# In each chunk of a state chain, the state's part of the outputs is multiplied in front of the solution instead of behind the remainders

## The chip, the cores and the metric

The kernel runs on one core of one Trainium2 chip. The metric is the device time of one execution in microseconds. Inputs and outputs are float32; matrices lie in DRAM and the output must agree with the reference below.

## The reference

One layer of a decoder trunk on a sequence of 1024 tokens with 1024 channels. Three branches (causal pooling, a delta-rule recurrence, cross-attention) share one input projection, are merged by gates and projected, and a feed-forward layer with a causal convolution follows. The change touches the recurrence alone:

```python
def rwkv7_scan(r, w, k, v, kk_neg, kk_a):
    ...
    def step(state, inp):
        rt, wt, kt, vt, an, bn = inp
        sa = jnp.einsum('bhvk,bhk->bhv', state, an)
        state = state * wt[:, :, None, :] + sa[..., None] * bn[:, :, None, :] + vt[..., None] * kt[:, :, None, :]
        yt = jnp.einsum('bhvk,bhk->bhv', state, rt)
        return state, yt
```

It runs for 16 heads of 64 channels. `state` is a 64x64 matrix for each head, and each token updates it and reads it.

## The kernel before

Channels lie on the 128 partitions and tokens along the free dimension. Projections are made with three matmuls of 128x512 for each pair of a weight block and an input block: operands are split into a high and a low part (`whi`, `wlo` for weights, `hh`, `hl` for the input), and `mm3` (L164) multiplies high by high (L167), high by low (L168) and low by high (L169) into a PSUM bank `psg`.

The recurrence runs over four groups of four heads (`rwkv_group`, L432). In a group, `i` (0, 1) counts blocks of 128 partitions, each with two heads: one on partitions 0 to 63 (`lo`), one on 64 to 127 (`up`). Tokens are cut into 16 chunks of 64. Preparation makes for each chunk a few 64x64 matrices: `AR` (scaled readers and keys), `NT` (the inverse of the chunk's triangular system), `RB` and `BKN`. Then the state chain (L645 to L691) goes through the chunks in order, and each step needs the state that the step before left in `HV`:

1. `pr`: four small matmuls of `AR` and `HV` give the remainders (right-hand sides) of the chunk's system, 128 rows deep and 64 columns wide (64 rows deep in the first chunk). VectorE copies them from PSUM to `Rs` (L662).
2. `py<-AR,HV`: from the second chunk on, four small matmuls give the state's part of the chunk's outputs, 64 rows deep and 64 columns wide. They open an accumulation in the PSUM tile `py`.
3. `pu<-Rs,NT`: four small matmuls, 64x64 as well, give the solution. VectorE copies the lower half to `HV` (L665), ScalarE the upper half (L666).
4. `ph<-HV,BKN`: four small matmuls for the next state, which VectorE adds to the decayed old one `Hd` into the next chunk's `HV` (L683) and again into `Hn` (L688), from which ScalarE makes the next `Hd` (L690).
5. `py<-RB,HV`: four small matmuls that complete the outputs; ScalarE copies `py` into `AR` (L691).

All these products are issued by `visit` (L636), so that line L639 stands for each of them in the profile; the tile names tell them apart. In the profile each of them appears as eight records, two for each of the four matmuls. `HV` of a chunk is complete before its `pr` starts, so `py<-AR,HV` waits for nothing that `pr` has not waited for.

The order of instructions on each engine is fixed when the program is built: a scheduler takes them by priority and data dependencies. `later` (L207) adds a dependency that sets this order but makes no engine wait, and `visit` chains its products with it, each behind the one before, the first behind `after`. Where the next small products are not ready yet by the scheduler's reckoning, it takes large matmuls of a projection that has no part in the chain: those of the next group's keys and values, or of the pooling, query and gate columns. So TensorE's queue in the chain is a mixture of rows of small products and single `psg` matmuls. PSUM tiles for `pr`, `pu` and `ph` come in turn from two banks (`bank`, L632), `py` from a pool of two.

Of the kernel before, what the change touches and what calls it, by code (L numbers as in the profile page):

```python
# [9 lines left out]
F32 = mybir.dt.float32  # L10
# [7 lines left out]
P = 128  # L18
# [3 lines left out]
C = 64  # L22
# [22 lines left out]
def trunk_kernel(ctx: ExitStack, tc: tile.TileContext, xT, memT, pvec, w_in, w_kv, w_upd, w_upg,  # L45
                 w_pool, w_ppool, w_pmem, w_prwkv, w_o, w_fup, w_fdn, out):
    nc = tc.nc
    V, A, G, PE, SP = nc.vector, nc.scalar, nc.gpsimd, nc.tensor, nc.sync
# [158 lines left out]
    def later(i, ins, plain=False):  # L207

        tc.add_manual_dep(i if plain else i.ins, ins.name, nosync, reason="order")
# [5 lines left out]
    rw = rw_ctx.enter_context(tc.tile_pool(name="rw", bufs=1))  # L215
# [7 lines left out]
    for k in range(KC):  # L223
        tag = ("X01", "X11", "HV", "HV")[k // 2]
# [207 lines left out]
    def rwkv_group(g, kv):  # L432
# [88 lines left out]
        NT = rw.tile([P, 2, NCH, C], F32, name="NT", tag="NT")  # L521
# [17 lines left out]
        for i in range(2):  # L539
            us = slice(NCH * i, NCH * i + NCH)  # L540
            for c0 in range(0, NCH, 4):
# [3 lines left out]
                lo, up = slice(0, 64), slice(64, 128)  # L545
# [81 lines left out]
        lo, up = slice(0, 64), slice(64, 128)  # L627
# [4 lines left out]
        def bank(name):  # L632
            turn[0] ^= 1
            return (psc if turn[0] else psk).tile([P, 2, C], F32, name=name, tag="c" if turn[0] else "k")

        def visit(products, after):  # L636

            for (out_, l, r), kw in products:
                m = PE.matmul(out_, l, r, **kw)  # L639
                if after is not None:  # L640
                    later(m, after)
                after = m.ins
            return after

        ready = None  # L645
        for c in range(NCH):
            t = slice(c * C, (c + 1) * C)
            once = dict(start=True, stop=True)
            pr = bank("pr")
            py = pss.tile([P, 2, C], F32, name="py", tag="s")  # L650
            ke, ko = (up, lo) if c == 0 else (slice(0, P), slice(0, P))
            row = []
            for i in range(2):
                row.append(((pr[up, i], AR[ko, i, 2, t], HV[ko, i, c, 1]), once))
                row.append(((pr[lo, i], AR[ke, i, 0, t], HV[ke, i, c, 0]), once))
            for i in range(2 if c else 0):
                kw = dict(start=i == 0, stop=False)
                row.append(((py[lo, i], HV[lo, i, c, 0], AR[lo, i, 1, t]), kw))
                row.append(((py[up, i], HV[up, i, c, 1], AR[up, i, 1, t]), kw))
            visit(row, ready)  # L660
            Rs = rw.tile([P, 2, C], F32, name="Rs", tag="Rs", bufs=1)
            V.tensor_copy(Rs, pr)  # L662
            pu = bank("pu")
            visit([((pu[q, i], NT[q, i, c], Rs[q, i]), once) for i in range(2) for q in (lo, up)], None)
            V.tensor_copy(HV[lo, :, c, 0], pu[lo])  # L665
            ready = A.copy(HV[up, :, c, 1], pu[up]).ins  # L666
            row = []
            if c + 1 < NCH:
                ph = bank("ph")
                for i in range(2):  # L670
                    row.append(((ph[up, i], BKN[i][:, c, 64:128], HV[:, i, c, 1]), once))
                    row.append(((ph[lo, i], BKN[i][:, c, 0:64], HV[:, i, c, 0]), once))
            for i in range(2):
                kw = dict(start=c == 0 and i == 0, stop=i == 1)
                row.append(((py[lo, i], HV[:, i, c, 0], RB[i][:, 0, c]), kw))
                row.append(((py[up, i], HV[:, i, c, 1], RB[i][:, 1, c]), kw))
            visit(row, ready)
            if c + 1 < NCH:
                for q, e in ((lo, 0), (up, 1)):
                    if c == 0:  # L680
                        ready = V.tensor_copy(HV[q, :, 1, e], ph[q]).ins
                    else:
                        ready = V.tensor_tensor(HV[q, :, c + 1, e], ph[q], Hd[q], op=ALU.add).ins  # L683
                if c + 2 < NCH:
                    if c == 0:
                        V.tensor_copy(Hn, ph)
                    else:
                        V.tensor_tensor(Hn, ph, Hd, op=ALU.add)  # L688
                    for i in range(2):
                        A.activation(Hd[:, i], Hn[:, i], AF.Identity, scale=Dc[:, i, c + 1:c + 2])  # L690
            A.copy(AR[:, :, 1, t], py)  # L691
# [40 lines left out]
    for g in range(4):  # L732
        kv = rwkv_group(g, kv)
# [113 lines left out]
    for hd in range(4):  # L847
        for t0, _ in HALVES:
            s = slice(t0, t0 + 512)
            q = as_.tile([P, 512], F32, name="q", tag="q", bufs=2)  # L850
# [5 lines left out]
            for u in range(2):  # L856
# [7 lines left out]
                pr = as_.tile([P, 2, 256], F32, name="prb", tag="prb", bufs=2)  # L864
# [742 lines left out]
```

## Time and profile before

| | us |
|---|---|
| median of 3 runs | 2088.79 |
| lowest and highest run | 2087.73, 2090.97 |
| span of the profiled execution | 2088.0 |
| first and last copy L662 (start in the span) | 236.4, 971.8 |

The profiled execution is one more execution; its span, from the first to the last instruction, is the time that the profile has for it. The four chains lie at about 236 to 311, 458 to 533, 681 to 756 and 902 to 975 us of it. Between them TensorE works on the preparation of the next group and on projections; the merge and the feed-forward layer come after the last.

In the profile, PE stands for TensorE's matmuls and PEld for its weight loads, DVE for VectorE, ACT for ScalarE, POOL for GpSimd. A row of a timeline has the start in us, the time from the first start to the last end, the engine, the line, the operation, output and operands by the program's names, the part of the array that is used (rows\*columns), and the shape. The end of a matmul is modelled and contains its way through the array, so that ends overlap the next starts; the time from start to start is what one costs in a full queue. What a row waited for stands in brackets behind it: "issue" is time in which the profile shows nothing waited for.

### The profile page before, as it was taken

The numbers are of one execution on the slowest core, as the hardware profiler recorded it, in microseconds if no ns is written. First come the engines' busy times: TensorE is split into PE (matmuls) and PEld (weight loads), VectorE is DVE, ScalarE is ACT, GpSimd is POOL, SyncE is SP. The second block draws the span as 40 slices with busy tenths as digits, with TensorE's granted clock in tenths as the row PEclk, the third lists the DMA queues.
The fourth block names the chain that finished last, engine by engine and source line by source line (L and its number), as shares of the span: only waits on it lengthen the run. The fifth ranks groups of instructions, "written<-read, shape, count | busy, mean of one in ns | idle before, by whom it ended". The sixth has DMA issues, their size and how long they took to land.

```text
span 2088.0 us, 34125 instructions
## 1 busy us (share of the span) xinstructions
PE 2032.2 (97%) x12246; PEld 1560.9 (75%) x12246; DVE 1358.1 (65%) x2167; ACT 1070.7 (51%) x2252; POOL 812.8 (39%) x917
## 2 busy tenths in 40 slices
PE   8999999999999999999999999998999999999997
PEld 5777767776778667876878878776788877777886
DVE  6567437654667357833695442669877777777798
ACT  7584348623773358434566243545444444444644
POOL 5521213121222121211122355565578888842341
PEclk9999999999999999999999999999999999999999
DMA  4312111120212021213526443634322222169766
GB/s 155 130 40 77 64 57 60 66 82 22 87 61 89 30 92 44 84 57 107 184 82 216 128 144 107 219 99 152 95 88 83 81 78 76 61 189 267 165 180 152
DMA packets 176713, 221.83 MB, mean 106 GB/s; under 512 B 16544, under 2 KB 128288, under 8 KB 176544
## 3 DMA queue, kind: packets, MB, share of 16 engines
q1 hardware_dynamic: 163616, 204.44, 30.1%
q0 software_dynamic: 11856, 14.16, 4.2%
q8 instruction: 97, 1.59, 0.3%
q10 hardware_dynamic: 1072, 1.05, 0.1%
q14 instruction: 72, 0.59, 0.1%
HBM read 170.30 MB, written 49.28 MB: 105 GB/s over the span
## 4 chain that ended last, share of the span: by engine, by line
PE 35%; DVE 5%; POOL 4%; DMA 4%; issue 3%; ACT 2%; SPq 1%; POOLq 0%; DVEq 0%; ACTq 0%
PE psg L167 6%; PE psg L168 6%; PE psg L169 6%; PE psf L169 2%; PE psf L168 2%; PE psf L167 2%; PE psd L168 2%; PE psd L169 2%; POOL wt L1025 2%; PE psd L167 2%; DMA R<-d_f 1%; DMA a<-in_w_fup 1%; POOL sm L1010 1%; ACT d L1041 1%; DVE d L1043 1%
## 5 line engine op out<-in xcount | busy, mean ns | idle before, releaser
L131 POOL TENSOR_TENSOR wlo<-wraw,whi 128x256 fp32r<-128x256 f32 x472 | 412.0, 882 | 955.4 <-ACT whi L128 770.0
L167 PE MATMUL psg<-hh,whi 128*128 128x512 f32 x928 | 382.7, 412 | 2.4 <-DVE kv L314 2.4
L169 PE MATMUL psg<-hh,wlo 128*128 128x512 f32 x928 | 379.4, 409 | 0.1
L168 PE MATMUL psg<-hl,whi 128*128 128x512 f32 x928 | 378.7, 408 | 0.0
L128 ACT CAST whi<-wraw 128x256 fp32r<-128x256 f32 x472 | 182.6, 403 | 231.3 <-PE psg L168 112.6
L167 PEld LDWEIGHTS psg<-hh,whi 128*128 128x128 f32 x928 | 174.4, 188 | 46.3 <-DVE kv L314 3.7
L169 PEld LDWEIGHTS psg<-hh,wlo 128*128 128x128 f32 x928 | 174.1, 188 | 46.1 <-POOL wlo L131 5.4
L168 PEld LDWEIGHTS psg<-hl,whi 128*128 128x128 f32 x928 | 174.4, 188 | 43.0 <-issue 3.6
L1025 POOL TENSOR_TENSOR wt<-a,wt 128x256 fp32r<-128x256 f32 x136 | 133.7, 1011 | 30.9 <-ACT wt L1024 30.9
L167 PE MATMUL psd<-f,u 128*128 128x512 f32 x292 | 115.2, 395 | 6.7 <-ACT f L1345 4.3
L168 PE MATMUL psd<-f,u 128*128 128x512 f32 x292 | 114.9, 394 | 0.9 <-DVE f L1349 0.9
L169 PE MATMUL psd<-f,u 128*128 128x512 f32 x292 | 114.2, 392 | 0.2 <-DVE u L1349 0.2
L1025 POOL TENSOR_TENSOR wt<-sm,wt 128x256 fp32r<-128x256 f32 x102 | 106.8, 1066 | 14.6 <-ACT wt L1024 14.6
L169 PE MATMUL psf<-h2h,wt 128*128 128x512 f32 x272 | 107.9, 397 | 0.1
L167 PE MATMUL psf<-h2h,wt 128*128 128x512 f32 x272 | 106.9, 393 | 0.1
L168 PE MATMUL psf<-h2l,wt 128*128 128x512 f32 x272 | 106.8, 393 | 0.0
L1024 ACT CAST wt<-sm 128x256 fp32r<-128x256 f32 x102 | 37.9, 404 | 128.0 <-POOL sm L1010 124.2
L1043 DVE SCALAR_TENSOR_TENSOR d<-z,pv,d 128x1023 f32<-128x1023 f32 x68 | 91.6, 1347 | 12.0 <-ACT d L1041 9.5
L169 PE MATMUL psf<-t,wt 128*128 128x512 f32 x204 | 81.5, 399 | 2.0 <-POOL wt L1025 1.9
L168 PE MATMUL psf<-t,wt 128*128 128x512 f32 x204 | 80.3, 394 | 0.0
L167 PE MATMUL psf<-t,wt 128*128 128x512 f32 x204 | 80.1, 393 | 0.0
L683 DVE TENSOR_TENSOR HV<-ph,Hd 64x128 f32<-64x128 f32 x112 | 32.3, 288 | 71.7 <-PE ph L639 47.6
(422 smaller groups left out, 4749.2 us busy)
## 6 DMA issues: line engine op xcount, KB each, us to landing
wraw<-in_w_in SPq DMA_DIRECT2D x240, 128.0 KB, 2.4
a<-in_w_fup SPq DMA_DIRECT2D x128, 128.0 KB, 2.4
d_zg<-st SPq DMA_DIRECT2D x48, 256.0 KB, 2.7
wraw<-in_w_fup SPq DMA_DIRECT2D x80, 128.0 KB, 2.4
fw<-in_w_fdn SPq DMA_DIRECT2D x33, 256.0 KB, 4.4
fraw<-d_f SPq DMA_DIRECT2D x33, 256.0 KB, 5.3
wraw<-in_w_prwkv SPq DMA_DIRECT2D x64, 128.0 KB, 2.4
wraw<-in_w_o SPq DMA_DIRECT2D x64, 128.0 KB, 2.5
```

Of the source, the lines that this page charges most:

```text
L128: last_whi[0] = A.copy(hi, src).ins
L131: (V if lo_on_dve[0] else G).tensor_tensor(lo, src, hi.bitcast(F32), op=ALU.subtract)
L167: first = PE.matmul(ps, wh, xh, start=start, stop=False)
L168: PE.matmul(ps, wh, xl, start=False, stop=False)
L169: last_mm[0] = PE.matmul(ps, wl, xh, start=False, stop=stop).ins
L683: ready = V.tensor_tensor(HV[q, :, c + 1, e], ph[q], Hd[q], op=ALU.add).ins
L1010: eng.tensor_tensor(out_[u], a[u], b[u], op=op)
L1024: A.copy(w[0][:, us], src[u])
L1025: last_low[0] = G.tensor_tensor(w[1][:, us], src[u], w[0][:, us].bitcast(F32), op=ALU.subtract).ins
L1041: A.activation(d, z, AF.Identity, scale=col("cw2", j), bias=col("cb", j))
L1043: V.scalar_tensor_tensor(d[:, n:], z[:, :T - n], col(cw, j), d[:, n:], op0=ALU.mult, op1=ALU.add)
```

## The change

The four products `py<-AR,HV` are taken out of the row of `pr` and put into the row of `pu`, ahead of it. The row of `pr` now ends with `pr`. The first product of the new row is ordered behind the copy `Rs` (`made`), as an order in the queue and not as a wait; `pu` is now chained behind `py`. In the first chunk, which has no `py<-AR,HV`, `pu` is ordered behind nothing, as before. No product, copy or transfer is added or taken away.

```diff
@@ -653,15 +653,17 @@
             for i in range(2):
                 row.append(((pr[up, i], AR[ko, i, 2, t], HV[ko, i, c, 1]), once))
                 row.append(((pr[lo, i], AR[ke, i, 0, t], HV[ke, i, c, 0]), once))
+            visit(row, ready)
+            Rs = rw.tile([P, 2, C], F32, name="Rs", tag="Rs", bufs=1)
+            made = V.tensor_copy(Rs, pr).ins
+            pu = bank("pu")
+            row = []
             for i in range(2 if c else 0):
                 kw = dict(start=i == 0, stop=False)
                 row.append(((py[lo, i], HV[lo, i, c, 0], AR[lo, i, 1, t]), kw))
                 row.append(((py[up, i], HV[up, i, c, 1], AR[up, i, 1, t]), kw))
-            visit(row, ready)
-            Rs = rw.tile([P, 2, C], F32, name="Rs", tag="Rs", bufs=1)
-            V.tensor_copy(Rs, pr)
-            pu = bank("pu")
-            visit([((pu[q, i], NT[q, i, c], Rs[q, i]), once) for i in range(2) for q in (lo, up)], None)
+            row += [((pu[q, i], NT[q, i, c], Rs[q, i]), once) for i in range(2) for q in (lo, up)]
+            visit(row, made if c else None)
             V.tensor_copy(HV[lo, :, c, 0], pu[lo])
             ready = A.copy(HV[up, :, c, 1], pu[up]).ins
             row = []
```

Line numbers behind L656 grow by two, so that L665, L666, L683 and L691 become L667, L668, L685 and L693; the copy `Rs` (L662) becomes L658.

The order of instructions changes on TensorE only; on the other engines the rows stand in the order of before. TensorE's queue in the second chunk of the first group, as 48 of the 60 chunks have it (`psg` is a large matmul of a projection, the rest are products of the chain):

```order
 L168 MATMUL psg<-hl,whi 128x512
 L639 MATMUL pr<-HV,AR 64x64 x4
+L169 MATMUL psg<-hh,wlo 128x512
 L639 MATMUL py<-AR,HV 64x64 x4
-L169 MATMUL psg<-hh,wlo 128x512
 L639 MATMUL pu<-Rs,NT 64x64 x4
 L167 MATMUL psg<-hh,whi 128x512
```

The large matmul that stood between `py` and `pu` now stands between `pr` and `py`, and `py` stands directly ahead of `pu`. In 12 chunks the scheduler has put four large matmuls there, since VectorE has a longer instruction (L314) ahead of the copy `Rs`. In six of them all four now stand ahead of `py`. TensorE's queue in one of the other six, in the first chain:

```order
 L169 MATMUL psg<-hh,wlo 128x512
 L639 MATMUL pr<-HV,AR 64x64 x4
+L167 MATMUL psg<-hh,whi 128x512
+L168 MATMUL psg<-hl,whi 128x512
+L169 MATMUL psg<-hh,wlo 128x512
 L639 MATMUL py<-AR,HV 64x64 x4
-L167 MATMUL psg<-hh,whi 128x512
-L168 MATMUL psg<-hl,whi 128x512
-L169 MATMUL psg<-hh,wlo 128x512
 L167 MATMUL psg<-hh,whi 128x512
 L639 MATMUL pu<-Rs,NT 64x64 x4
```

Here three large matmuls have moved ahead of `py`, and the fourth stands between `py` and `pu`.

## The prediction

> **What bounds the kernel now.** The page comes first: which engine is full, and whether it is full all the way.
>
> ```profile
> PE 2032.2 (97%) x12246; PEld 1560.9 (75%) x12246; DVE 1358.1 (65%) x2167; ACT 1070.7 (51%) x2252; POOL 812.8 (39%) x917
> ...
> PE   8999999999999999999999999998999999999997
> ```
>
> TensorE is busy for 97% of the span and in the tens of nines almost everywhere; VectorE is at 65%, ScalarE at 51%. So time is saved by whatever makes TensorE's own queue shorter, as long as nothing else becomes late. The change sits in the state chain, which runs four times. The view of busy time by stretch shows the first two of them (237 to 312 and 470 to 535) and the stretch that follows the second:
>
> ```profile
> core 0: us, PE busy (x) PEld busy (x) DVE busy (x) ACT busy (x) POOL busy (x), PEclk, DMA share, GB/s
> ...
> 237.00:312.00 75.00, 75.00 (x949) 50.34 (x949) 26.32 (x87) 28.90 (x84) 8.02 (x11) 1.00 0.12 43
> ...
> 470.00:535.00 65.00, 65.00 (x731) 43.20 (x726) 24.89 (x84) 26.55 (x80) 8.02 (x11) 1.00 0.13 46
> 535.00:680.00 145.00, 142.41 (x795) 108.92 (x795) 105.03 (x172) 88.82 (x169) 35.77 (x43) 1.00 0.22 73
> ```
>
> In the chain PE is busy for all of the time (75.00 of 75.00 us, 65.00 of 65.00), at the full granted clock, with VectorE and ScalarE at about a third to two fifths. A busy PE is not yet a PE that does useful work without gaps, since the ends of matmuls are modelled. So the starts have to be read. This is the timeline of PE alone over one chunk of the first chain (`pr`, `py` from `AR,HV`, `pu`, `ph`, `py` from `RB,HV` are the chain's products, four matmuls in eight records each; `psg` is a large matmul of an unrelated projection that fills the queue):
>
> ```profile
> 297.13 0.39 PE L168 MATMUL psg<-hl,whi 128*128 128x512 f32 x1
> 297.36 0.40 PE L169 MATMUL psg<-hh,wlo 128*128 128x512 f32 x1
> 297.69 0.45 PE L639 MATMUL ph<-HV,BKN 128*64 128x64 f32 x8
> 297.97 0.40 PE L639 MATMUL py<-RB,HV 128*64 128x64 f32 x8
> 298.30 0.50 PE L167 MATMUL psg<-hh,whi 128*128 128x512 f32 x1
> 298.64 0.40 PE L168 MATMUL psg<-hl,whi 128*128 128x512 f32 x1
> 299.01 0.45 PE L639 MATMUL pr<-HV,AR 128*64 128x64 f32 x8
> 299.39 0.45 PE L639 MATMUL py<-AR,HV 64*64 64x64 f32 x8
> 299.77 0.49 PE L169 MATMUL psg<-hh,wlo 128*128 128x512 f32 x1
> 300.19 0.45 PE L639 MATMUL pu<-Rs,NT 64*64 64x64 f32 x8
> 300.57 0.50 PE L167 MATMUL psg<-hh,whi 128*128 128x512 f32 x1
> ```
>
> The reader should subtract each start from the next. `psg` behind `psg` of the same kind takes 0.23 us (297.13 to 297.36). `ph` gives way to `py<-RB,HV` after 0.28, and that one to `psg` after 0.33: 0.61 for the two. But `pr` takes 0.38 until `py<-AR,HV`, that takes 0.38 until `psg`, and `pu` takes 0.38. The column behind the tile names tells why: 128\*64, 64\*64 and 128\*128 are the part of the array that an instruction uses. Where this shape changes from one row to the next, eight records cost 0.38; where it stays (`ph`, `py<-RB,HV`, both 128\*64) 0.28. So **a change of shape costs such a row 0.10 us at its end (0.38 against 0.28) and 0.05 at its start (0.38 against 0.33).** That it is the shape and not the kind of operand is seen where a plain product and a projection meet in one shape:
>
> ```profile
> 311.41 0.40 PE L169 MATMUL psg<-hh,wlo 128*128 128x512 f32 x1
> 311.65 1.02 PE L707 MATMUL pvar<-yq,bonesr 128*128 128x512 f32 x2
> 312.11 0.80 PE L167 MATMUL psg<-hh,whi 128*128 128x512 f32 x1
> ```
>
> `pvar` comes 0.24 us behind `psg` and its two records take 0.46, 0.23 each: no gap on either side. The weight loads say the same:
>
> ```profile
> 297.69 0.31 PEld L639 LDWEIGHTS ph<-HV,BKN 128*64 128x64 f32 x8 [0.36 <-issue]
> 297.91 0.32 PEld L639 LDWEIGHTS py<-RB,HV 128*64 128x64 f32 x8
> 298.30 0.19 PEld L167 LDWEIGHTS psg<-hh,whi 128*128 128x128 f32 x1
> ```
>
> At a change of shape the first load starts only with its matmul (297.69, 298.30); inside one shape it starts ahead (297.91, for a matmul at 297.97, while `ph` runs until 298.14).
>
> **The change part by part.** It adds and removes no instruction. In 60 chunks (all but the first of each chain) `py<-AR,HV` moves from directly behind `pr` to behind the large matmuls; the rows of the other engines stand in the order they had. In 48 chunks one `psg` stands between `pr` and `pu`, in 12 there are four. In 54 chunks `py` comes directly ahead of `pu`, both 64\*64; in 6 of the 12 one `psg` gets between them.
>
> *The 48 chunks.* Before: 300.57 - 299.01 = 1.56 us from `pr` to the `psg` behind `pu` (0.38 + 0.38 + 0.42 + 0.38). After it needs four prices. `pr` to `psg` I read in the first chunk, where they already meet (there `pr` is 64\*64):
>
> ```profile
> 235.93 0.45 PE L639 MATMUL pr<-HV,AR 64*64 64x64 f32 x8
> 236.31 0.51 PE L167 MATMUL psg<-hh,whi 128*128 128x512 f32 x1
> ```
>
> 0.38, as at every other change of shape. The lone `psg` then costs 0.42, as now ahead of `pu` (299.77 to 300.19). `py` to `pu` is shown nowhere in this trace. Its bounds are 0.28 (two rows of one shape, `ph` and `py<-RB,HV`) and 0.38 (a row that starts afresh). I take 0.28: both are 64\*64, they use the same two parts of the array in the same turn, and the nearest row is the pair of one shape. Then `pu` to `psg` is 0.33, as behind `py<-RB,HV`. Sum 0.38 + 0.42 + 0.28 + 0.33 = 1.41, a gain of 0.15; with 0.38 for both open steps it is 1.56, a gain of nothing.
>
> The Trainium skill, TensorEngine Tiling (Array Packing), section Key Properties, says that the array is drained when the tiling mode changes, and not when only the tile within a mode does. The prices of 0.38 and 0.28 above agree with it; by this rule `py` to `pu` is 0.28 and the gain 0.15, without it the pair could stand at 0.38 and the gain at nothing.
>
> *The 12 chunks with four large matmuls.* One of them:
>
> ```profile
> 303.03 0.45 PE L639 MATMUL pr<-HV,AR 128*64 128x64 f32 x8
> 303.41 0.45 PE L639 MATMUL py<-AR,HV 64*64 64x64 f32 x8
> 303.79 0.50 PE L167 MATMUL psg<-hh,whi 128*128 128x512 f32 x1
> 304.12 0.39 PE L168 MATMUL psg<-hl,whi 128*128 128x512 f32 x1
> 304.35 0.40 PE L169 MATMUL psg<-hh,wlo 128*128 128x512 f32 x1
> 304.59 0.39 PE L167 MATMUL psg<-hh,whi 128*128 128x512 f32 x1
> 304.91 0.45 PE L639 MATMUL pu<-Rs,NT 64*64 64x64 f32 x8
> 305.29 0.50 PE L168 MATMUL psg<-hl,whi 128*128 128x512 f32 x1
> ```
>
> Before: 305.29 - 303.03 = 2.26. In the six where `py` joins `pu`: 0.38 + 0.33 + 0.23 + 0.24 + 0.32 + 0.28 + 0.33 = 2.11, again 0.15 gained. In the six where a `psg` stands between them: `pr` 0.38, two `psg` 0.33 + 0.23, the third 0.32 ahead of `py`, `py` 0.38, the lone `psg` 0.42, `pu` 0.38: 2.44. One more change of shape, and 0.18 lost.
>
> *The wait of `pu`.* `pu` needs the copy `Rs`, which VectorE makes from `pr`. Until now `py` and a `psg` hid that copy; now the `psg` and `py` do, the same work in the other order, but 0.1 us shorter. This is VectorE over that chunk:
>
> ```profile
> 298.25 0.61 DVE L683 TENSOR_TENSOR HV<-ph,Hd 64x128 f32<-64x128 f32 x2 [1.30 <-PE ph L639]
> ...
> 299.50 0.29 DVE L662 COPY Rs<-pr 128x128 f32<-128x128 f32 x1 [0.31 <-PE pr L639]
> ```
>
> The copy ends at 299.79. How long TensorE takes to see an end of VectorE's has a bound in the start of `pr`, which waits for L683: its end is 298.86 and `pr` starts at 299.01, 0.15 later. So `Rs` can be used from 299.94 on. `pu` will be due at 299.01 + 0.38 + 0.42 + 0.28 = 300.09, and its first load about 0.06 ahead of that (as 297.91 is of 297.97), at 300.03. The cover holds by 0.09 us. If it did not, `pu` would start late, and what is queued behind it on TensorE (the next four `psg`, then `ph`) would be late too. In the 12 chunks VectorE comes to `Rs` later but the four matmuls leave far more room. What follows `pu` (the copies L665 and L666, `ph`, L683) keeps its distance from `pu`.
>
> *The sum.* 54 x 0.15 = 8.1 us gained, 6 x 0.18 = 1.1 us lost: **7.0 us less**, 0.34%. Against the profiled execution's span of 2088.0 that is 2081.0; the median of the runs shown is 2088.79, 0.8 above the span, and the forecast is put on it: **2081.8 us**. Rounding in the rows (0.01 in each difference) is worth about 0.6 us of it.
>
> **The rivals.** *A. `pu` starts afresh.* Its weights go to the same rows of the array that `py` is using; if they can't be loaded while `py` runs, `py` to `pu` costs 0.38 and `pu` to `psg` 0.38. Then 54 chunks gain nothing and six lose 0.18: +1.1, or 2089.9 us. For it: nowhere in this trace do two rows of 64\*64 meet. Against it: `py<-RB,HV` at 297.91 is loaded into the rows that `ph` is still using, and within one row of eight the loads overlap as well (eight in 0.31 us, from a row that is 0.45 long). The Trainium skill, TensorE: Matmul & The Clock Gate, section The mechanism, states in one place that a weight load overlaps a running matmul only if it goes to another group of rows; by that rule A would hold, and the loads just named disagree with it.
>
> *B. The wait breaks the pair, and the kernel gets slower.* The place is the first load of `pu`, which carries the wait for `Rs`. If TensorE looks at it only when `py` has run out, the pair falls apart as in A, and a look at the semaphore comes on top. Its price is that of `pr`, which waits on VectorE too: `psg` to `pr` takes 0.37 (298.64 to 299.01), `psg` to `ph` 0.33 (297.36 to 297.69), so 0.04. 54 x 0.04 + 1.1 = +3.3, or 2092.1 us. It decides from the point where `Rs` is seen more than 0.09 us later than I bound it, or where a met wait costs something. Against it: the first product of `ph` needs the copy L666 of ScalarE and the second one L665 of VectorE, a wait in the middle of the row, and still `py<-RB,HV` follows after 0.28.
>
> *C. The gain is given back later.* Between the chains PE is idle for some us (142.41 of 145.00 busy, 535 to 680), waiting for VectorE and ScalarE. If part of that work ends by something that doesn't follow TensorE, an earlier end of the chain only makes a wait longer. With half of the gain gone: 2085.3 us. Against it: the longest waits of PE are far from the chain and small.
>
> ```profile
> PE psn L1094 <- DVE s L1089: 8.6, 1, 8.6
> PE px L262 <- DVE xsq L261: 5.0, 1, 5.0
> PE psd L167 <- ACT f L1345: 4.3, 3, 2.9
> ...
> PE pr L639 <- DVE HV L683: 0.3, 1, 0.3
> ```
>
> The first is one wait behind all four chains, the second lies ahead of them, and none grows with an earlier start of the engine that it waits for.
>
> **How the numbers follow.** Forecast 0.75 (own range 2079.8 to 2083.8: the rounding, and the 3.2 us between the lowest and the highest run shown); A 0.11; C 0.08; B 0.05; anything else 0.01. The range has to take in both ends of the step that no row shows, from all 60 chunks gaining (2079.8) to A (2089.9): 2079.5 to 2090.0. It leaves out B, and little else. About 0.2%, 4.2 us, is what a measurement of this kernel can tell from no change. Faster by more than that: the forecast and a small part of C, 0.77. Within it: A, most of C and part of B, 0.18. Slower: the rest, 0.05.
>
> **What would show it.** In the profile after, in chunks of one `psg`: `pr` to `psg` 0.38, `psg` to `py` 0.42, `py` to `pu` 0.28, `pu` to `psg` 0.33, and a whole chunk of 3.87 us where it is 4.02 now (starts of `pr`: 299.01 less 294.99). In A `py` to `pu` reads 0.38. In B a wait of `pu` for `Rs` L658 appears among PE's waits. In C the chain stretches are shorter and the stretches between them longer by as much. The prediction falls if a row of 64\*64 behind another of 64\*64 drains, or if `Rs` arrives behind `py`.

## The result and the profile after

| | before | after |
|---|---|---|
| median of 5 runs, us | 2090.10 | 2082.64 |
| lowest and highest, us | 2087.73, 2092.08 | 2078.99, 2084.65 |
| ratio, 95% interval | | 0.9964 (0.9953 to 0.9975) |
| span of the profiled execution, us | 2088.0 | 2082.7 |

The changed kernel is 0.36% faster: 7.5 us between the medians, where 7.0 us were forecast. The busy shares of the page hardly tell it:

```profile
PE 2026.5 (97%) x12246; PEld 1559.1 (75%) x12246; DVE 1358.2 (65%) x2167; ACT 1070.6 (51%) x2252; POOL 810.8 (39%) x917
```

VectorE and ScalarE do what they did, and PE has 5.7 us less. The view of busy time by stretch shows the first chain as full as before:

```profile
237.00:312.00 75.00, 75.00 (x964) 50.17 (x961) 26.78 (x88) 29.96 (x86) 8.03 (x11) 1.00 0.14 44
```

75.00 us busy of 75.00 both times, but with 964 matmul records in place of 949. The difference is seen only from start to start, in PE's timeline of one chunk:

```profile
294.72 0.45 PE L639 MATMUL pr<-HV,AR 128*64 128x64 f32 x8
295.10 0.50 PE L168 MATMUL psg<-hl,whi 128*128 128x512 f32 x1
295.54 0.45 PE L639 MATMUL py<-AR,HV 64*64 64x64 f32 x8
295.82 0.40 PE L639 MATMUL pu<-Rs,NT 64*64 64x64 f32 x8
296.15 0.50 PE L169 MATMUL psg<-hh,wlo 128*128 128x512 f32 x1
```

`pr` to `psg` 0.38, `psg` to `py` 0.44 (0.43 in the mean of the 48 chunks), `py` to `pu` 0.28, `pu` to `psg` 0.33: 1.43 us where it was 1.56, in a chunk that now takes 3.86 us in place of 4.02. And one of the six chunks in which a large matmul stands between the two:

```profile
302.44 0.45 PE L639 MATMUL pr<-HV,AR 128*64 128x64 f32 x8
...
303.71 0.45 PE L639 MATMUL py<-AR,HV 64*64 64x64 f32 x8
304.09 0.51 PE L167 MATMUL psg<-hh,whi 128*128 128x512 f32 x1
304.52 0.45 PE L639 MATMUL pu<-Rs,NT 64*64 64x64 f32 x8
304.90 0.50 PE L168 MATMUL psg<-hl,whi 128*128 128x512 f32 x1
```

2.46 us from `pr` to the `psg` behind `pu`; it was 2.26. Where the time went is measured best on the chains themselves, from the first `pr` to the last. The last one of the first chain before (where the first starts at 235.93):

```profile
307.72 0.45 PE L639 MATMUL pr<-HV,AR 128*64 128x64 f32 x8
```

and the first and last after (of the first row the view shows three records):

```profile
236.99 0.32 PE L639 MATMUL pr<-HV,AR 64*64 64x64 f32 x3
...
307.35 0.45 PE L639 MATMUL pr<-HV,AR 128*64 128x64 f32 x8
```

71.79 us became 70.36. Over the four chains together this measure falls from 284.96 to 278.61, by 6.35 us. It holds 56 of the 60 chunks, of which 50 are joined and six split: 50 x 0.15 - 6 x 0.18 = 6.4. The three stretches between the chains kept their length (450.4 and 450.1 us together, each with the last chunk of a chain in it, which gains 0.15), so nothing was given back there. What lies behind the last `pr` varies by itself: two executions of the changed kernel had 1117.1 and 1111.4 us there, and 278.61 and 278.64 in the chains. The chains can be compared to a tenth of a microsecond, the whole only to some microseconds.

### The profile page after: what moved, and what is told of

Read it like the earlier page. It is cut to its first block, busy times and chain, and to the rows that moved or that the text cites. A ratio compares the mean times of both kernels' runs of the same rounds, so it can differ in the third digit from the quotient of the medians.

```text
span 2082.7 us, 34125 instructions
## 1 busy us (share of the span) xinstructions
PE 2026.5 (97%) x12246; PEld 1559.1 (75%) x12246; DVE 1358.2 (65%) x2167; ACT 1070.6 (51%) x2252; POOL 810.8 (39%) x917
## 4 chain that ended last, share of the span: by engine, by line
PE 36%; DVE 5%; DMA 4%; POOL 3%; issue 2%; ACT 2%; SPq 1%; POOLq 0%; ACTq 0%; DVEq 0%
PE psg L167 6%; PE psg L169 6%; PE psg L168 6%; PE psf L169 3%; PE psf L167 3%; PE psf L168 3%; POOL wt L1027 2%; PE psd L168 2%; PE psd L169 2%; PE psd L167 2%; DMA R<-d_f 1%; POOL sm L1012 1%; DMA a<-in_w_fup 1%; ACT d L1043 1%; DMA fw<-in_w_fdn 1%
## 5 line engine op out<-in xcount | busy, mean ns | idle before, releaser
L128 ACT CAST whi<-wraw 128x256 fp32r<-128x256 f32 x472 | 182.7, 403 | 227.9 <-PE psg L168 122.1
L685 DVE TENSOR_TENSOR HV<-ph,Hd 64x128 f32<-64x128 f32 x112 | 32.3, 289 | 71.8 <-PE ph L639 47.7
```

The costliest lines, as they stand in the source:

```text
L128: last_whi[0] = A.copy(hi, src).ins
```

## The experiments

**The theory** is the one of the forecast: a row of small matmuls pays about 0.15 us where the array's shape changes, and the change takes away one such change in 54 chunks. **The rival** is the place: `py` may be cheap ahead of `pu` because of what it hides there (the copy `Rs`) or because of what its weight loads meet. Shape and place were varied apart. Each table row is compared with the kernel before on the same chip (medians of before: 2087.19 for the first four, 2086.28 for the next three, 2087.33 for the last two); "chains" is the sum from the first `pr` to the last over the four chains, 284.96 before.

| run | us | ratio (95% interval) | chains, us |
|---|---|---|---|
| wide_py_front | 2079.11 | 0.9960 (0.9947 to 0.9972) | 276.56 |
| wide_py_late | 2088.46 | 1.0006 (0.9997 to 1.0015) | 286.52 |
| joined | 2079.89 | 0.9965 (0.9952 to 0.9977) | 278.49, 6 `psg` more |
| changed_again | 2079.71 | 0.9965 (0.9953 to 0.9978) | 278.64 |
| narrow_pr | 2077.97 | 0.9962 (0.9950 to 0.9975) | 276.42 |
| crossed_py | 2069.14 | 0.9917 (0.9904 to 0.9931) | 268.52 |
| pu_first | 2081.61 | 0.9976 (0.9965 to 0.9986) | 303.67, 108 `psg` more |
| crossed_py_front | 2087.92 | 1.0004 (0.9995 to 1.0013) | 285.07 |
| crossed_pu | 2069.07 | 0.9914 (0.9901 to 0.9928) | 268.13, 9 `psg` more |

**Another shape in the old place, and in the new place.** Both have the same edit, the first in the kernel before and the second in the changed one:

```diff
-                row.append(((py[lo, i], HV[lo, i, c, 0], AR[lo, i, 1, t]), kw))
-                row.append(((py[up, i], HV[up, i, c, 1], AR[up, i, 1, t]), kw))
+                row.append(((py[lo, i], HV[:, i, c, 0], AR[:, i, 1, t]), kw))
+                row.append(((py[up, i], HV[:, i, c, 1], AR[:, i, 1, t]), kw))
```

> The kernel before, with py<-AR,HV still directly behind pr, but 128 rows deep (it takes both halves of HV and AR, so that a foreign term is added and the outputs are not the reference's). Only the shape of py changes, from 64*64 to 128*64, which is the shape of pr. Theory, change of shape: pr to py falls from 0.38 to 0.28 us and py to psg from 0.38 to 0.33 in all 60 chunks, -0.15 x 60 = -9.0 us, ratio 0.9957, without any move. Rival, place (the gain comes from where py stands, by what it hides or by what its weights' loads meet): the time of before, ratio 1.000, and pr to py stays at 0.38.

> The changed kernel, with py<-AR,HV ahead of pu, but 128 rows deep as in the run before (outputs not the reference's). Place as in the changed kernel, shape unlike that of pu. Theory, change of shape: py to pu reads 0.38 us and pu to psg 0.38, so the 54 joined chunks cost what they cost before and the six split ones 0.18 more: +1.1 us, ratio 1.0005. Rival, place: the gain of the changed kernel stays, about -7 us, ratio 0.9966, and py to pu reads 0.28.

PE's timeline of the first, with `py` behind `pr`:

```profile
291.36 0.45 PE L639 MATMUL pr<-HV,AR 128*64 128x64 f32 x8
291.61 0.43 PE L639 MATMUL py<-AR,HV 128*64 128x64 f32 x8
291.98 0.50 PE L167 MATMUL psg<-hh,whi 128*128 128x512 f32 x1
```

0.25 and 0.37 us, 0.62 for the two in place of 0.76. The sum is the one expected, the two steps are not (0.28 and 0.33 were), and no run shows why it falls apart in this way. Nothing was moved, and the chains are 8.4 us shorter (56 x 0.15 = 8.4), with 8.1 us on the median. PE's timeline of the second, with `py` ahead of `pu` but of another shape:

```profile
293.65 0.45 PE L639 MATMUL py<-AR,HV 128*64 128x64 f32 x8
294.03 0.45 PE L639 MATMUL pu<-Rs,NT 64*64 64x64 f32 x8
294.41 0.50 PE L168 MATMUL psg<-hl,whi 128*128 128x512 f32 x1
```

0.38 and 0.38: the place is that of the changed kernel and the whole gain is gone, the chains 1.6 us longer than before. The shape decides, the place does not.

**The neighbour's shape.** Here `py` is left alone and `pr` gets its shape, in the kernel before:

```diff
-            ke, ko = (up, lo) if c == 0 else (slice(0, P), slice(0, P))
+            ke, ko = (up, lo) if c == 0 else (lo, up)
```

> The kernel before, with py<-AR,HV directly behind pr, but pr 64 rows deep in all chunks (it leaves out the half of the contraction that takes the chunk's values, and keeps the half that takes the state, so that the chain's dependencies stay). pr is then 64*64, as py is. Theory, change of shape: pr to py 0.28 us, py to psg 0.33, in all 60 chunks, -0.15 x 60 = -9.0 us, ratio 0.9957. Rival, place: pr to py stays at 0.38, time of before.

The chains are 8.5 us shorter and the median 8.3 us: as expected from the third side. `pr` to `py` took 0.25 us and `py` to `psg` 0.36, the sum as in the run with the wide `py`.

**The six split chunks.**

```diff
-            row += [((pu[q, i], NT[q, i, c], Rs[q, i]), once) for i in range(2) for q in (lo, up)]
-            visit(row, made if c else None)
+            sol = [((pu[q, i], NT[q, i, c], Rs[q, i]), once) for i in range(2) for q in (lo, up)]
+            swap = g < 3 and c in (8, 14)
+            visit(sol + row if swap else row + sol, made if c else None)
```

> The changed kernel, but in the six chunks in which a large matmul comes between py and pu, pu is put in front of py, so that the two stand next to each other in all 60 chunks. Theory, change of shape: these six gain 0.15 us each instead of losing 0.18, 2.0 us less than the changed kernel, -9.0 us against before, ratio 0.9957; pu to py reads 0.28 there. Rival, place (py has to stand ahead of pu): no gain over the changed kernel, -7 us, ratio 0.9966.

> The changed kernel once more, beside the others on one chip: -6.7 to -7.5 us against before by the theory of the change of shape (54 x 0.15 gained, 6 x 0.18 lost is 7.0; the runs so far gave 7.5), ratio 0.9964 to 0.9968; the same by any other theory.

The changed kernel came out at 0.9965 again. The joined one did not beat it. The pairs themselves did what was expected: the six chunks take 4.81 us with five large matmuls between `pr` and the pair, where they took 4.91 with four there, so 0.33 less each when the additional one is counted at 0.23. But from the first `pr` to the last of the fourth chain the joined kernel needs 728.1 us and the changed one 728.7: of the 2.0 us expected 0.6 are left there, too little for the medians to show.

The traces show two places where the rest was lost. In one more chunk of each of the first three chains a weight cast on ScalarE (L128) now stands ahead of the copy of the solution's upper half (now L669), `ph` waits for that copy, and the chunk is 0.2 us longer: 0.6 in all. And behind each of these chains weights come late by 0.7 us, for instance:

```profile
359.83 0.50 PE L169 MATMUL psg<-hh,wlo 128*128 128x512 f32 x1 [0.70 <-POOL wlo L131]
```

That the two large matmuls taken in earlier shift the need for weights is the likely reason, but it was not tested. In the first two stretches this costs nothing in the end, because a longer wait of the changed kernel is gone there, that of `pv` (a product of the next group's preparation) for ScalarE:

```profile
371.68 0.27 PE L528 MATMUL pv<-cent,kv 64*64 64x64 f32 x1 [1.04 <-ACT HV L531]
```

The third stretch had no such wait. With its two large matmuls less it should be 0.46 us shorter than in the changed kernel, and it is 0.65 longer.

**`pu` in front everywhere.**

```diff
-            visit(row, made if c else None)
+            visit(sol + row, made if c else None)
```

> The changed kernel with pu in front of py in all 60 chunks. The scheduler then puts three large matmuls between pr and pu where one stood (five in place of four in some), so that the chain takes in more of the projections. Theory, change of shape: pu to py 0.28 us and py to psg 0.33 in all 60, -9.0 us; in the last chunk of each chain py<-RB,HV is split in two by a psg, one more change back and forth, about +0.2 x 4 = 0.8, so -8.2 us, ratio 0.9961, unless weights for the additional projections come late, as they do by 0.7 us in three places where pu stands in front in six chunks: then about -6, ratio 0.997. Chains longer in time by about 2 x 0.23 us in each chunk. Rival, cover (py has to stand ahead of pu to hide the copy Rs): pu waits for Rs, slower than the changed kernel by the wait, 48 x 0.1, ratio 0.999.

All 60 pairs cost 0.28 and 0.33, and yet the kernel is not ahead of the changed one. Its ratio is 0.0011 higher (2.3 us), a difference that the two intervals do not tell from none; 1.2 us less than the changed kernel were expected. The late weights that the expectation allowed for are not among PE's waits in and between the chains. Nor is it the rival: no wait of `pu` for `Rs` appears, since the scheduler puts three large matmuls ahead of it. What waits more often is `ph`, for the copy of the solution's upper half (now L668) on ScalarE. The timeline of one such place on ScalarE, and PE's weight load that waits for it:

```profile
253.40 0.41 ACT L128 CAST whi<-wraw 128x256 fp32r<-128x256 f32 x1 [1.28 <-PE psg L168]
...
253.83 0.26 ACT L668 COPY HV<-pu 64x128 f32<-64x128 f32 x1
...
254.15 0.31 PEld L639 LDWEIGHTS ph<-HV,BKN 128*64 128x64 f32 x8 [0.52 <-ACT HV L668]
```

A weight cast stands ahead of the copy, and the weight loads stand idle for 0.52 us before `ph`, where 0.36 is usual. Over the 56 chunks that have a `ph`, the step from `psg` to `ph` is 2.4 us longer in sum than in the changed kernel. This does not settle the whole time. From the first `pr` to the last, pu_first needs 733.4 us and the changed kernel 728.7, but 30 more large matmuls lie inside, worth about 6.9 us at 0.23 each; so up to there it is not behind. What it may lose behind the last `pr`, where the time varies by some microseconds from one execution to the next, stays open.

**The same shape, other parts of the array.** This was to tell the shape from the parts that an instruction uses. In the changed kernel, and afterwards in the kernel before:

```diff
-                row.append(((py[lo, i], HV[lo, i, c, 0], AR[lo, i, 1, t]), kw))
-                row.append(((py[up, i], HV[up, i, c, 1], AR[up, i, 1, t]), kw))
+                row.append(((py[up, i], HV[lo, i, c, 0], AR[lo, i, 1, t]), kw))
+                row.append(((py[lo, i], HV[up, i, c, 1], AR[up, i, 1, t]), kw))
```

> The changed kernel, but py<-AR,HV uses the two other 64*64 parts of the array (rows of one half into columns of the other, which swaps the two heads' state terms in the outputs), so that pu, next to it, works in the same shape but not in the same parts. Theory, change of shape: only the shape counts, py to pu stays at 0.28 us and the time at that of the changed kernel, -7.0 us, ratio 0.9966. Rival, same parts: the pair is cheap only because both use the same parts of the array; then py to pu reads 0.38 and the gain goes, +1.1 us, ratio 1.0005.

Neither theory had this: 17 us less than before, 10 less than the changed kernel. The timeline shows the two rows no longer one behind the other but interleaved, so that eight products run in the time of four. If that is the cause, the crossing must be worth nothing where `py` has no neighbour of its shape, and as much if `pu` is crossed in place of `py`. The latter leaves nothing out of the computation:

```diff
-            row += [((pu[q, i], NT[q, i, c], Rs[q, i]), once) for i in range(2) for q in (lo, up)]
+            row += [((pu[o, i], NT[q, i, c], Rs[q, i]), once) for i in range(2) for q, o in ((lo, up), (up, lo))]
...
-            V.tensor_copy(HV[lo, :, c, 0], pu[lo])
-            ready = A.copy(HV[up, :, c, 1], pu[up]).ins
+            V.tensor_copy(HV[lo, :, c, 0], pu[up])
+            ready = A.copy(HV[up, :, c, 1], pu[lo]).ins
```

> The kernel before, with py<-AR,HV directly behind pr as there, but in the two other 64*64 parts of the array (the two heads' state terms in the outputs are swapped). Theory, four parts at once: the crossed run gained 10 us over the changed kernel because py and pu, in different parts, ran at the same time; here py has no neighbour of its shape, so nothing is gained, time of before, ratio 1.000, py to psg 0.38 us. Rival, the crossing itself (other PSUM or SBUF partitions are cheaper): a gain here too, some -10 us, ratio 0.995.

> The changed kernel, with pu instead of py in the two other parts: the solution of one half of the partitions is written to the other half in PSUM, and the copies into HV bring it back, so that nothing of the computation is left out. By the order of the program py and pu are neighbours in all 60 chunks here, and in some chunks two more large matmuls come in behind. Theory, four parts at once: py and pu together take 0.41 us until the next psg, as in the crossed run, where the changed kernel takes 0.61: 60 x 0.20 = 12.0 on top of 60 x 0.15 = 9.0, -21 us against before, ratio 0.990; at least the -17 of the crossed run, ratio 0.9917. Rival, the crossed copies cost more (reading one half of the partitions and writing the other): copies longer than 0.28 and 0.26 us and later, ph waits for them, ratio 0.994 or more.

Behind `pr` the crossing is worth nothing (1.0004, chains 285.07). With `pu` crossed the kernel is 18.3 us faster than before. PE's timeline of one of its chunks:

```profile
296.58 0.45 PE L639 MATMUL pr<-HV,AR 128*64 128x64 f32 x8
296.96 0.50 PE L168 MATMUL psg<-hl,whi 128*128 128x512 f32 x1
297.40 0.27 PE L639 MATMUL py<-AR,HV 64*64 64x64 f32 x2
297.42 0.27 PE L639 MATMUL pu<-Rs,NT 64*64 64x64 f32 x2
297.50 0.23 PE L639 MATMUL py<-AR,HV 64*64 64x64 f32 x2
...
297.65 0.22 PE L639 MATMUL pu<-Rs,NT 64*64 64x64 f32 x2
297.80 0.50 PE L169 MATMUL psg<-hh,wlo 128*128 128x512 f32 x1
```

From `py` to the next `psg` 0.40 us, where the changed kernel takes 0.61. It beats both kernels of this case. The run with the crossed `py`, whose outputs have two heads' terms swapped, is as fast within the intervals. The crossed copies themselves cost next to nothing: VectorE's takes 0.29 us in place of 0.28, ScalarE's 0.26 as before. Of the 21 us expected, 18 came. Of the rest, 1.2 us lie in the step from `psg` to `ph`, which waits in some chunks for ScalarE's copy behind a weight cast, as in pu_first. Three waits of 0.7 us for weights appear as in the joined kernel, but two waits of 1.0 us of `pv` are gone in turn, so they don't explain the remainder; it stays open.

## Why the prediction was right

*What bounds the kernel.* Right for this change: TensorE's queue was the bound in the chains, and what was taken from it came out of the whole time.

*The price of a change of shape.* Right, and shown by the three runs that changed a shape and left the place, or kept the place and changed the shape back. The Trainium skill, TensorEngine Tiling (Array Packing), section Key Properties, has it as a rule (a change of tiling mode drains the array, another tile of one mode does not); the runs agree, and give it a size here: 0.15 us for one change less.

One reading on the way to it was wrong, without harm. The two records of `pvar` do not take 0.23 us each: in the trace of before the `psg` behind them starts 0.46 us after `pvar` (312.11), but the next one only at

```profile
312.75 0.40 PE L168 MATMUL psg<-hl,whi 128*128 128x512 f32 x1
```

0.64 us later, where `psg` behind `psg` takes 0.23. So `pvar` costs 0.46 + 0.41 = 0.87 us, some 0.43 for each record. A group of four of them a little later takes 1.32 + 0.40 = 1.72, twice as much, so that "no gap on either side" stands. That it is the shape and not the kind of operand rests better on the runs with the wide `py` and the narrow `pr`, where the step from `pr` to `py`, both plain products, fell from 0.38 to 0.25.

*The step that no row showed,* `py` to `pu`, was put at 0.28 out of 0.28 to 0.38: it measured 0.28 in all 54 chunks, and `pu` to `psg` 0.33. The wait that `pu` carries cost nothing, so that the rivals A and B both fell. The weight loads of the changed kernel, in the chunk shown above:

```profile
295.53 0.31 PEld L639 LDWEIGHTS py<-AR,HV 64*64 64x64 f32 x8 [0.24 <-issue]
295.76 0.32 PEld L639 LDWEIGHTS pu<-Rs,NT 64*64 64x64 f32 x8
```

The first load of `pu` starts at 295.76, ahead of its matmul (295.82), while `py` runs until 295.99 by its modelled end. For A the rule in TensorE: Matmul & The Clock Gate, section The mechanism, of the Trainium skill (loads run ahead only into other rows) would have had to hold; `py` and `pu` use the same rows, and the loads ran ahead. That no rows of 64\*64 meet in the trace of before is true of the chain only: outside it the products `pv` (L528 and L529), 64\*64 as well, stand one behind the other from 372.40 to 373.22, a pair of records every 0.06 us without a break.

*The reason given for 0.28* was partly beside the point. The forecast named two things, one shape and the same two parts of the array. The crossed runs show that the same parts are no help: they are what keeps `py` and `pu` one behind the other.

*The six split chunks* lose 0.2 us each, forecast 0.18.

*What follows `pu`* did not quite keep its distance, as the forecast had it: `pu` to `psg` fell from 0.38 to 0.33, so that `ph` comes 0.05 us sooner behind `pu`. The copies were still in time; the step from the last `psg` to `ph` is 0.33 us in the mean in both kernels.

*The cover of `Rs`* was larger than forecast. The bound of 0.15 us from an end on VectorE to a start on TensorE was taken from `pr`. In the crossed kernel, VectorE's timeline has the copy at

```profile
297.07 0.29 DVE L658 COPY Rs<-pr 128x128 f32<-128x128 f32 x1 [0.31 <-PE pr L639]
```

and `pu` starts at 297.42, 0.06 behind its end. So the cover in the changed kernel is about 0.09 us wider than the 0.09 that were forecast. This is seen in the changed kernel itself: in the chunk shown above the copy ends at 295.50, 0.26 us ahead of the first load of `pu`.

*Rival C*, the gain given back between the chains, did not happen in the changed kernel (450.4 and 450.1 us there). In the joined one most of the additional gain was lost, in part behind the third chain, with a wait for late weights in it, and in part inside the chains, at a copy behind a weight cast; the forecast named neither.

*The size.* 7.0 us forecast, 6.35 us measured on 56 of the 60 chunks; the four that lie outside that measure, all of them joined, make it about 6.9. The 7.5 us between the medians agree within their interval (5.2 to 9.8 us), which is too wide to tell 7.0 from 6.

## What to carry to other kernels

Where rows of small matmuls are mixed with large ones, count how often the array's shape changes from one row to the next, and put rows of one shape next to each other: each change less was worth 0.15 us here, though TensorE read as fully busy all the time. Then let neighbours of one shape use different parts of the array; that was worth another 0.2 us for each pair, and asked of the code only that the copies read the other half of the partitions. A scheduler that fills the queue reacts to such a move: where it drew large matmuls ahead, copies came behind weight casts and weights came late, and the joined kernel kept 0.6 of 2.0 us.

## What the runs showed of the hardware that was not expected

Two rows of eight 64\*64 records ran at the same time when they used different parts of the array: 0.40 us for both, where one alone costs 0.38 and two in the same parts 0.61. The Trainium skill, TensorEngine Tiling (Array Packing), section Key Properties, has the rule for it (different tiles can load weights and multiply in parallel). The two rows alternate although all of `py` is ordered ahead of `pu`: the first records of `pu` start at 297.42, ahead of the third of `py` at 297.50. An end on VectorE was seen by TensorE 0.06 us later at most (297.36 to 297.42 in the crossed kernel).
